# Delta rule of a decoder step: the scale rows of k and q go through DRAM instead of one-hot products

## The chip, the cores and the metric

The kernel runs on one core of a Trainium2 chip. The metric is the device time of one execution in microseconds (us); the kernel is timed several times and the median is given. One execution was taken by the hardware profiler. In the profile PE is TensorE's matmul stream, PEld its weight loads, DVE is VectorE, ACT ScalarE, POOL GpSimd and SP SyncE, which issues most of the transfers (SPq in the rows is its queue, POOLq that of GpSimd). 1% of the time is about 19 us.

## The reference, cut to what matters

One step of a two-layer decoder for a prompt of 256 tokens and 32 sample tokens (8 requests of 4). Each layer has a token mixer with three branches, of which one is a gated delta rule with 8 heads; the lines that matter here scale k and q by one number for each token and head:

```
q = l2norm(qkv[:, :, 0]) * (DN_DK ** -0.5)
k = l2norm(qkv[:, :, 1])
...
kb = kc * bc[..., None]
a_mat = jnp.einsum('bihd,bjhd->bhij', kb, kc) * jnp.where(strict, decay, 0.0)
...
q_dec = jnp.moveaxis(qc * jnp.exp(gcum)[..., None], 1, 2)
scores = jnp.einsum('bihd,bjhd->bhij', qc, kc) * decay
```

## The kernel before, in words

Activations lie with channels on the 128 partitions and the T = 288 tokens (256 and 32) in the free dimension. Nearly all the work is projections: 128x128 weight tiles, each split into a high and a low part, so that a tile is three products with 288 columns. These are the rows `mmps<-xh,wh`, `mmps<-xl,wh` and `mmps<-xh,wl`. Four tiles form one block: SP loads it (`wr<-in_wst`, 256 KB, 6 buffers), ACT writes its high part (`wh<-wr`), DVE its low part (`wl<-wr,wh`), two blocks ahead of TensorE; `wh` and `wl` have 4 buffers. A layer has 450 blocks.

Everything else is written as generators that run in the background: each time that a block begins (`w`, `tick`), the first two generators of a list advance to their next `yield`; `yield n` sits out n of these turns. A scheduler then gives every engine a fixed order of instructions, with waits for data and for free buffers. Tiles of 128x288 (`self.A`) come from one pool of 50 buffers.

The delta rule of four heads is one generator, `dn_mix(hf)`, with hf = 0 and 1, so four passes in two layers. Here they are called pass 0 and pass 1 of a layer. A pass first has its eight scale factors for each token and head in a tile with tokens on partitions (`TK`), turns them by transposes into 32 rows of 288 tokens (`rows`), copies these to SBUF (`fr`, `stack`) and splits them into two parts in a 128-partition tile (`st`, shown as `dst`). Rows h, 4 + h and 8 + h are the factors of k, of q and of the decayed q of head h; row 12 + h holds the summed log decay.

To multiply a head's k (128 channels x 288 tokens) by a row of tokens, the row has to stand on all partitions. `bcast` does that with a product: the stationary operand is one column of a one-hot matrix, repeated 128 times, the moving one is `st`, and the result is a PSUM tile `rowbc` with the row on every partition. DVE then multiplies k or q by it (`kq<-k,rowbc`, `kq<-q,rowbc`, `qd<-q,rowbc`). `kq`, with one buffer, is the moving operand of the products `pk`. Each of four heads has three such products and one of the same form for row 12 + h, which a mask product (`rowbc<-msk,idb`) is added to and ACT exponentiates (`et`, `eg`). PSUM tiles for all of this come from five banks (`self.X`).

Of the kernel before, what the change touches and what calls it, by code (L numbers as in the profile page):

```python
# [8 lines left out]
F32 = mybir.dt.float32  # L9
# [8 lines left out]
P = 128  # L18
TP = 256
TS = 32  # L20
T = TP + TS
# [204 lines left out]
class Net:  # L226
# [344 lines left out]
    def spread(self, r, w=72):  # L571
        bc = self.X("bc")
        for g in range(4):
            self.mmul(bc[:, w * g:w * g + w], self.ident[:, 32 * g:32 * g + 1].to_broadcast([P, P]), r)
        return bc
# [232 lines left out]
    def stack(self, psrow, n, tag, bufs, again=False):  # L808
        st = self.St[tag]
        s0 = st  # L810
        if again:
            st = s0[:, 128:128 + T]
        fr = self.A(nm="fr")[0:32]
        fs = self.R([32, 32], tag + "s", bufs=bufs)
        if n < 32:
            self.nc.gpsimd.memset(fr, 0.0)
        self.cp(fr[0:n], psrow[0:n, 0:T])
        self.cp(st[0:32], fr)
        self.tt(st[32:64], fr, st[0:32].bitcast(F32), ALU.subtract)
        self.pcp(fs, fr[:, 256:288])  # L820
        if again:
            self.vcp(s0[0:64, 0:128], st[0:64, 128:256].bitcast(F32))
        return s0, fs

    def bcast(self, st, m):
        ps = self.X("rowbc")
        self.mmul(ps[:, 0:T], self.e32[:, m:m + 1].to_broadcast([P, P]), st)
        return ps


    def dn_proj(self, hf, xs, out):
# [13 lines left out]
    def dn_mix(self, hf, q, k, v):  # L845
# [46 lines left out]
        ps = self.X("vtr")  # L892
# [5 lines left out]
        rows = self.X("rows")  # L898
        for c in range(2):
            self.tp(rows[0:32, c * 128:c * 128 + 128], TK[:, c].rearrange("p a h -> p (a h)"))  # L900
        self.mmul(rows[0:32, 256:288], TK[0:32, 2].rearrange("p a h -> p (a h)"), self.ident[0:32, 0:32])
        st, fr = self.stack(rows, 32, "dst", 1)
        yield 1
        ps = self.X("vtr")
        for h in range(4):
            self.tp(ps[:, h * 128:h * 128 + 128], v[h][:, 128:256])
        for h in range(4):
            self.act(r4(vb[1])[:, h], r4(ps)[:, h], AF.Copy, scale=TK[:, 1, 6, h:h + 1])
        yield

        av = lambda t: t.rearrange("p (a i) -> p a i", a=2)
        m = self.M(1024, nm="asc")
        ASC = [[av(self.A(nm="asc")[:, 0:256]) for _ in range(4)], [av(m[:, i * 256:i * 256 + 256]) for i in range(4)]]
        asc = lambda c, h: ASC[c][h]
        QD = self.R([P, 4, 160], "qd")
        KQ = self.R([P, 4, 2, 32], "kqs")
        EG = self.R([P, 4, 9], "eg", bufs=2)
        for h in range(4):
            kq = self.R([P, 2, T], "kq")
            b0 = self.bcast(st, h)  # L920
            self.tt(kq[:, 0, :], k[h], b0[:, 0:T])
            b1 = self.bcast(st, 4 + h)
            self.tt(kq[:, 1, :], q[h], b1[:, 0:T])
            gb = self.X("rowbc")
            sel = self.e32[:, 12 + h:13 + h].to_broadcast([P, P])

            self.mmul(gb[:, 0:T], sel, st, True, False)
            self.mmul(gb[:, 0:256], self.idb, self.MK("mk3")[:, 0:256], False, True)
            et = self.S(256, "et")
            for c in range(2):  # L930
                self.act(et[:, c * 128:c * 128 + 128], gb[:, c * 128:c * 128 + 128], AF.Exp,
                         bias=G[:, 5, c, hf * 4 + h:hf * 4 + h + 1])
            self.act(EG[:, h, 0:1], gb[:, 255:256], AF.Exp)
            self.act(EG[:, h, 1:9], gb[:, 256:288].rearrange("p (b s) -> p b s", s=4)[:, :, 3], AF.Exp)
            yield
            b2 = self.bcast(st, 8 + h)
            self.tt(QD[:, h], q[h][:, 128:288], b2[:, 128:288])
            pk = self.X("pk")
            pkv = pk.rearrange("p (c a i) -> p c a i", c=2, a=2)
            for c in range(2):  # L940
                self.mmul(pkv[:, c], k[h][:, c * 128:c * 128 + 128], kq[:, :, c * 128:c * 128 + 128])
            for c in range(2):
                self.stt(asc(c, h), pkv[:, c], TK[:, c, 4, h:h + 1],
                         et[:, c * 128:c * 128 + 128].unsqueeze(1).to_broadcast([P, 2, P]))
            self.pcp(KQ[:, h], kq[:, :, 256:288])
            yield
# [4 lines left out]
        for b in range(2):  # L951
            ps = self.X("atr")
# [36 lines left out]
        for c in range(2):  # L989
            ps = self.X("ktr")  # L990
# [87 lines left out]
        ps = b4()  # L1078
# [5 lines left out]
        ps = b4()  # L1084
# [8 lines left out]
        for j in range(2):  # L1093
            po = self.X("po").rearrange("p (h t) -> p h t", h=2)
            for i in range(2):
                h = 2 * j + i
# [5 lines left out]
        ps = b4()  # L1102
# [13 lines left out]
        ps = self.X("on")  # L1116
# [225 lines left out]
    def ssm_rows(self):  # L1342
        G = self.gtok
        while (self.l, "scalars") not in self.done:
            yield
        rows = self.X("rows")
        for c in range(2):
            self.tp(rows[0:16, c * 128:c * 128 + 128], G[:, 0, c, 8:24])
        self.mmul(rows[0:16, 256:288], G[0:32, 0, 2, 8:24], self.ident[0:32, 0:32])
        st, fr = self.stack(rows, 16, "sst", 1, again=True)  # L1350
        el = self.S(8, "sel")
        yield
        ea = self.X("ea")
        for g in range(4):
            self.mmul(ea[32 * g:32 * g + 32, 0:16], fr[0:16], self.C("i32")[0:16, 0:16])
        EA = self.R([P, 16], "sea")
        self.act(EA, ea[:, 0:16], AF.Exp)
        self.act(el[0:16], fr[0:16].rearrange("p (b s) -> p b s", s=4)[:, :, 3], AF.Exp)
        yield
        ed = self.S(128, "eld")[0:16].rearrange("p (b h) -> p b h", b=NB)  # L1360
        self.tt(ed, el[0:16].unsqueeze(2).to_broadcast([16, NB, 16]),
                self.C("i32")[0:16, 0:16].unsqueeze(1).to_broadcast([16, NB, 16]))
        yield
        elp = self.X("elp")
        self.mmul(elp[:, 0:128], self.ones[0:16], ed)
        EL = self.R([P, NB, 16], "sel2")
        self.cp(EL, elp[:, 0:128].rearrange("p (b h) -> p b h", b=NB))
        self.sst = (st, EA, EL)
# [704 lines left out]
```

## Time and profile before

| | us |
|---|---|
| median of 3 runs | 1889.24 |
| lowest and highest | 1888.33, 1892.48 |
| the profiled execution, its own time | 1886.77 |
| span of the profiled execution, first to last instruction | 1884.9 |
| PE busy | 1857.6 (99%) |
| DVE busy | 1404.7 (75%) |
| ACT busy | 1126.6 (60%) |
| POOL busy | 307.2 (16%) |

The mean granted clock of TensorE is 0.998 of full speed. The 1.9 us between time and span lie around the span. A matmul's row lasts longer than the distance to the next one's start, since matmuls overlap: what one costs is read from the starts.

### The profile page before, as it was taken

The numbers are of one execution on the slowest core, as the hardware profiler recorded it, in microseconds if no ns is written. First come the engines' busy times: TensorE is split into PE (matmuls) and PEld (weight loads), VectorE is DVE, ScalarE is ACT, GpSimd is POOL, SyncE is SP. The second block draws the span as 40 slices with busy tenths as digits, with TensorE's granted clock in tenths as the row PEclk, the third lists the DMA queues.
The fourth block names the chain that finished last, engine by engine and source line by source line (L and its number), as shares of the span: only waits on it lengthen the run. The fifth ranks groups of instructions, "written<-read, shape, count | busy, mean of one in ns | idle before, by whom it ended". The sixth has DMA issues, their size and how long they took to land. (4 is left out here: it accounts for less than half of the span.)

```text
span 1884.9 us, 44571 instructions
## 1 busy us (share of the span) xinstructions
PE 1857.6 (99%) x16446; PEld 1733.4 (92%) x16446; DVE 1404.7 (75%) x3153; ACT 1126.6 (60%) x2735; POOL 307.2 (16%) x777
## 2 busy tenths in 40 slices
PE   9999999999999999999999999999999999999998
PEld 8998999988999989999999889989889999899997
DVE  6978767677978768766588785777688887587665
ACT  6666665655546457756466756656655465476563
POOL 3533212332000000000024232123210000000000
PEclk9999999999999999999999999999999999999999
DMA  7545446588554684766556453465876556747663
GB/s 257 173 147 170 120 118 196 164 286 275 186 172 145 206 289 138 239 202 205 152 158 182 121 180 111 132 200 158 294 265 187 171 171 208 253 153 239 213 191 98
DMA packets 184442, 354.52 MB, mean 188 GB/s; under 512 B 30688, under 2 KB 42144, under 8 KB 184224
## 3 DMA queue, kind: packets, MB, share of 16 engines
q1 hardware_dynamic: 176320, 326.44, 55.6%
q0 software_dynamic: 7904, 25.23, 3.8%
q8 instruction: 129, 2.11, 0.5%
q14 instruction: 89, 0.73, 0.1%
HBM read 316.54 MB, written 35.05 MB: 187 GB/s over the span
## 5 line engine op out<-in xcount | busy, mean ns | idle before, releaser
L294 ACT CAST wh<-wr 128x512 fp32r<-128x512 f32 x900 | 555.4, 620 | 553.5 <-PE mmps L286 467.7
L303 DVE TENSOR_TENSOR wl<-wr,wh 128x512 fp32r<-128x512 f32 x900 | 619.2, 691 | 285.0 <-ACT wh L294 272.2
L286 PE MATMUL mmps<-xh,wh 128*128 128x288 f32 x2400 | 725.7, 305 | 4.3 <-DVE xh L307 1.8
L286 PE MATMUL mmps<-xl,wh 128*128 128x288 f32 x2400 | 712.2, 297 | 0.0
L286 PE MATMUL mmps<-xh,wl 128*128 128x288 f32 x2400 | 709.2, 296 | 0.2 <-DVE wl L303 0.2
L286 PEld LDWEIGHTS mmps<-xh,wh 128*128 128x128 f32 x2400 | 450.6, 189 | 24.2 <-issue 12.3
L286 PEld LDWEIGHTS mmps<-xl,wh 128*128 128x128 f32 x2400 | 453.1, 189 | 9.0 <-issue 5.6
L286 PEld LDWEIGHTS mmps<-xh,wl 128*128 128x128 f32 x2400 | 452.4, 188 | 6.4 <-issue 3.8
L286 PE MATMUL mmps<-prs,wh 128*128 128x288 f32 x1280 | 260.5, 297 | 0.7 <-ACT prs L294 0.6
L286 PEld LDWEIGHTS mmps<-prs,wh 128*128 128x128 f32 x1280 | 205.3, 188 | 2.2 <-ACT prs L294 0.9
L286 PE MATMUL mmps<-prs,wl 128*128 128x288 f32 x640 | 188.5, 295 | 0.0
L312 DVE SCALAR_TENSOR_TENSOR cy<-cb,cwh,cy 128x312 f32<-128x312 f32 x240 | 129.5, 540 | 19.8 <-ACT cy L291 13.5
L286 PEld LDWEIGHTS mmps<-prs,wl 128*128 128x128 f32 x640 | 120.7, 189 | 0.0
L286 PE MATMUL mmps<-ph,wh 128*128 128x288 f32 x256 | 76.4, 298 | 0.0
L286 PE MATMUL mmps<-pl,wh 128*128 128x288 f32 x256 | 75.7, 296 | 0.0
L286 PE MATMUL mmps<-ph,wl 128*128 128x288 f32 x256 | 75.6, 295 | 0.0
L331 POOL DMA_DIRECT2D out_osd<-dnu x32 | 17.3, 542 | 338.6 <-DVE dnu L312 330.3
L300 POOL COPY cvp<-cb 128x3 f32<-128x3 f32 x80 | 29.6, 370 | 214.0 <-ACT cb L294 213.8
L291 ACT ACTIVATE ct<-cy 128x312 f32<-128x312 f32 x80 | 37.3, 466 | 37.8 <-DVE cy L312 34.3
L286 PEld LDWEIGHTS mmps<-ph,wh 128*128 128x128 f32 x256 | 48.1, 188 | 2.1 <-ACT b L294 0.8
L286 PEld LDWEIGHTS mmps<-pl,wh 128*128 128x128 f32 x256 | 48.1, 188 | 0.8 <-issue 0.4
L286 PEld LDWEIGHTS mmps<-ph,wl 128*128 128x128 f32 x256 | 48.1, 188 | 0.4 <-issue 0.4
(509 smaller groups left out, 2941.4 us busy)
## 6 DMA issues: line engine op xcount, KB each, us to landing
wr<-in_wst SPq DMA_DIRECT2D x900, 256.0 KB
kc<-in_k SPq DMA_DIRECT2D x28, 512.0 KB
kc<-in_v SPq DMA_DIRECT2D x28, 512.0 KB
dns<-in_dns SPq DMA_DIRECT2D x16, 512.0 KB
h<-in_h SPq DMA_DIRECT2D x16, 512.0 KB
out_oss<-h POOLq DMA_DIRECT2D x16, 512.0 KB, 3.8
kc<-in_km SPq DMA_DIRECT2D x16, 512.0 KB
kc<-in_vm SPq DMA_DIRECT2D x16, 512.0 KB
```

The lines of the kernel that those rows point to most:

```text
L286: self.nc.tensor.matmul(out, lhsT, rhs, start=start, stop=stop)
L291: return self.nc.scalar.activation(out, in_, func, **k)
L294: self.nc.scalar.copy(out, in_)
L300: self.nc.gpsimd.tensor_copy(out, in_)
L303: self.nc.vector.tensor_tensor(out, a, b, op=op)
L312: return self.nc.vector.scalar_tensor_tensor(out, a, s, b, op0=op0, op1=op1)
L331: self.nc.gpsimd.dma_start(out=out, in_=in_)
```

## The change

`bcast` is gone. After `stack` (which now also returns `fr`) the first 12 rows of `fr` are stored to a DRAM tile `dr` by POOL's queue, and each row is loaded from there with a source step of 0 over the partitions, so that all 128 partitions of an SBUF tile `rb` get the same 1152 bytes. `spread(h)` issues the three loads of head h: those of heads 0 and 1 ahead of the loop over heads, those of heads 2 and 3 in the turns of heads 0 and 1. DVE's three multiplications read `rb` in SBUF instead of `rowbc` in PSUM. The fourth product, for the log decay, stays. Ahead of the loop, `yield` becomes `yield 1`: the loop starts one turn, so one block, later.

```diff
-    def bcast(self, st, m):
-        ps = self.X("rowbc")
-        self.mmul(ps[:, 0:T], self.e32[:, m:m + 1].to_broadcast([P, P]), st)
-        return ps
...
-        st, fr = self.stack(rows, 32, "dst", 1)
+        st, fr, full = self.stack(rows, 32, "dst", 1)
+        dr = self.pd.tile([12, T], F32, tag="dr", name="dr")
+        self.store(dr, full[0:12])
+        rb = {}
+
+        def spread(h):
+            for m in range(h, 12, 4):
+                rb[m] = self.A(nm="rb")
+                self.load(rb[m], bass.AP(dr.tensor, dr.offset + m * T, [[0, P], [1, T]]))
         yield 1
+        spread(0)
         ps = self.X("vtr")
...
-        yield
+        spread(1)
+        yield 1
...
-            b0 = self.bcast(st, h)
-            self.tt(kq[:, 0, :], k[h], b0[:, 0:T])
-            b1 = self.bcast(st, 4 + h)
-            self.tt(kq[:, 1, :], q[h], b1[:, 0:T])
+            self.tt(kq[:, 0, :], k[h], rb.pop(h))
+            self.tt(kq[:, 1, :], q[h], rb.pop(4 + h))
...
-            b2 = self.bcast(st, 8 + h)
-            self.tt(QD[:, h], q[h][:, 128:288], b2[:, 128:288])
+            self.tt(QD[:, h], q[h][:, 128:288], rb.pop(8 + h)[:, 128:288])
+            if h < 2:
+                spread(h + 2)
```

TensorE's order in pass 0 of layer 1, at the turn from head 0 to head 1. Before:

```order
L286 MATMUL mmps<-xh,wh 128x288
L286 MATMUL mmps<-xl,wh 128x288
L286 MATMUL pk<-kq,k 128x256 x2
L286 MATMUL rowbc<-dst,e_439 128x288 x3
L286 LDWEIGHTS idb
L286 MATMUL rowbc<-msk,idb 128x256
L286 MATMUL mmps<-xh,wl 128x288
```

The same place in the order of the change:

```order
L286 MATMUL mmps<-xh,wl 128x288
L286 MATMUL pk<-kq,k 128x256 x2
L286 MATMUL rowbc<-dst,e_439 128x288
L286 LDWEIGHTS idb
L286 MATMUL rowbc<-msk,idb 128x256
L286 MATMUL mmps<-xh,wh 128x288
```

Two of the three products with `dst` are gone here (the third, for the decayed q, stood alone further down and is gone too). The first `rowbc` of the pass now stands 5 projection products later than before, and 33 projection products lie between it and head 0's `pk`; before it was 19, with one more `rowbc` among them.

VectorE's order at head 0 of the same pass. Before:

```order
L303 TENSOR_TENSOR dst<-fr,dst 32x288
L312 SCALAR_TENSOR_TENSOR cy<-cb_125,cwh,cy 128x312
L303 TENSOR_TENSOR wl<-wr,wh 128x512
L312 SCALAR_TENSOR_TENSOR cy<-cb_125,cwh,cy 128x312
L303 TENSOR_TENSOR wl<-wr,wh 128x512
L303 TENSOR_TENSOR kq<-k,rowbc 128x288
L312 SCALAR_TENSOR_TENSOR k<-ct,cy 128x256
L303 TENSOR_TENSOR kq<-q,rowbc 128x288
L303 TENSOR_TENSOR wl<-wr,wh 128x512
L303 TENSOR_TENSOR qd<-q,rowbc 128x160
```

And in the change:

```order
L303 TENSOR_TENSOR dst<-fr,dst 32x288
L312 SCALAR_TENSOR_TENSOR cy<-cb_125,cwh,cy 128x312
L303 TENSOR_TENSOR wl<-wr,wh 128x512
L312 SCALAR_TENSOR_TENSOR cy<-cb_125,cwh,cy 128x312
L303 TENSOR_TENSOR wl<-wr,wh 128x512
L312 SCALAR_TENSOR_TENSOR k<-ct,cy 128x256
L303 TENSOR_TENSOR wl<-wr,wh 128x512 x3
L303 TENSOR_TENSOR kq<-k,rb 128x288
L303 TENSOR_TENSOR kq<-q,rb 128x288
L303 TENSOR_TENSOR wl<-wr,wh 128x512
L303 TENSOR_TENSOR qd<-q,rb 128x160
```

The two multiplications of head 0 have moved behind three more `wl` of later blocks.

SyncE's queue in the same pass; before, 21 weight loads stood in one run here:

```order
L328 DMA wr<-in_wst 128x512 x12
L328 DMA rb<-dr 128x288 x6
L328 DMA wr<-in_wst 128x512 x3
L328 DMA rb<-dr 128x288
L328 DMA wr<-in_wst 128x512
L328 DMA rb<-dr 128x288 x2
L328 DMA wr<-in_wst 128x512 x2
L328 DMA rb<-dr 128x288 x2
L328 DMA wr<-in_wst 128x512
L328 DMA rb<-dr 128x288
```

The twelve loads of a pass stand between weight loads, six of them in one run.

## Rows read from the trace of the kernel before

**Rows 1.** The page: busy time, share of the span and instructions.

```profile
PE 1857.6 (99%) x16446; PEld 1733.4 (92%) x16446; DVE 1404.7 (75%) x3153; ACT 1126.6 (60%) x2735; POOL 307.2 (16%) x777
```

**Rows 2.** Waits on TensorE, all places: us, times, longest.

```profile
PE rowbc L286 <- DVE dst L303: 0.4, 2, 0.2
```

**Rows 3.** Layer 1's passes 0 and 1: PE, PEld, DVE, ACT, POOL, clock, DMA, GB/s.

```profile
141.00:165.00 24.00, 23.60 (x166) 22.00 (x165) 21.91 (x56) 17.34 (x55) 9.12 (x26) 1.00 0.39 114
262.00:286.00 24.00, 23.84 (x171) 21.94 (x170) 19.09 (x50) 13.93 (x47) 5.24 (x12) 1.00 0.40 119
```

**Rows 4.** Instructions on tile rowbc: durations min/median/max in ns.

```profile
L286 PE MATMUL rowbc<-dst,e x64: 288/294/482, 146.5 to 1216.8; 128*128 128x288 f32 x64
L303 DVE TENSOR_TENSOR kq<-k,rowbc x16: 439/454/455, 148.6 to 1214.5; 128x288 f32<-128x288 f32 x16
```

**Rows 5.** Timeline of PE, pass 0 of layer 1, head 2: start, length.

```profile
155.19 0.29 PE L286 MATMUL mmps<-xh,wl 128*128 128x288 f32 x1
155.32 0.56 PE L286 MATMUL rowbc<-dst,e 128*128 128x288 f32 x3
155.72 0.28 PE L286 MATMUL rowbc<-msk,idb 128*128 128x256 bf16 x1
...
157.42 0.30 PE L286 MATMUL rowbc<-dst,e 128*128 128x288 f32 x1
157.56 1.02 PE L286 MATMUL pk<-kq,k 128*128 128x256 f32 x4
```

**Rows 6.** Timeline of PE at head 0 of layer 1's passes 0 and 1.

```profile
146.02 0.29 PE L286 MATMUL mmps<-xh,wh 128*128 128x288 f32 x1
146.51 0.67 PE L286 MATMUL rowbc<-dst,e 128*128 128x288 f32 x3 [0.21 <-DVE dst L303]
...
264.37 0.29 PE L286 MATMUL mmps<-xh,wl 128*128 128x288 f32 x1
264.82 1.10 PE L286 MATMUL pk<-kq,k 128*128 128x256 f32 x4 [0.15 <-DVE sst L297]
```

**Rows 7.** Timeline of ACT and POOL in pass 0 of layer 1.

```profile
144.25 0.39 ACT L294 COPY fr<-rows 32x288 f32<-32x288 f32 x1
...
144.81 0.20 POOL L300 COPY dsts<-fr 32x32 f32<-32x32 f32 x1
```

**Rows 8.** The DMA view and tile xd: us from issue to landing (last number).

```profile
out_ocs<-cvo POOLq DMA_DIRECT2D x4, 144.0 KB, 2.1
...
out_ocp<-cvp POOLq DMA_DIRECT2D x8, 6.0 KB, 3.5
...
DMA to landing us min/median/max: 2.0/4.0/6.3
```

**Rows 9.** Timeline of SP's queue and ACT at the kernel's start.

```profile
1.18 0.42 SPq L328 DMA_DIRECT2D x<-in_x  x1
1.65 0.42 SPq L328 DMA_DIRECT2D wr<-in_wst  x1
...
3.90 0.53 ACT L291 ACTIVATE xh<-x,prm 128x288 fp32r<-128x288 f32 x1 [1.57 <-DMA x<-in_x]
```

**Rows 10.** Timeline of DVE at head 0, pass 0 of layer 1.

```profile
146.95 0.69 DVE L303 TENSOR_TENSOR wl<-wr,wh 128x512 fp32r<-128x512 f32 x1
...
148.01 0.69 DVE L303 TENSOR_TENSOR wl<-wr,wh 128x512 fp32r<-128x512 f32 x1
148.61 0.45 DVE L303 TENSOR_TENSOR kq<-k,rowbc 128x288 f32<-128x288 f32 x1
149.00 0.43 DVE L312 SCALAR_TENSOR_TENSOR k<-ct,cy 128x256 f32<-128x256 f32 x1
149.35 0.45 DVE L303 TENSOR_TENSOR kq<-q,rowbc 128x288 f32<-128x288 f32 x1
```

**Rows 11.** What SP's queue waits for, the longest: us, times, longest.

```profile
SPq L328 <- DVE wl L303: 1033.2, 697, 11.2
```

**Rows 12.** Instructions on tile kqs: POOL's copies of kq.

```profile
L300 POOL COPY kqs<-kq x16: 236/636/1196, 149.9 to 1215.4; 128x64 f32<-128x64 f32 x16
```

More of the change, by code (lines that the diff above doesn't have):

```diff
@@ L822, in stack @@
             self.vcp(s0[0:64, 0:128], st[0:64, 128:256].bitcast(F32))
-        return s0, fs
-    def bcast(self, st, m):
-        ps = self.X("rowbc")
-        self.mmul(ps[:, 0:T], self.e32[:, m:m + 1].to_broadcast([P, P]), st)
-        return ps
+        return s0, fs, fr
     def dn_proj(self, hf, xs, out):
@@ L1349, in ssm_rows @@
         self.mmul(rows[0:16, 256:288], G[0:32, 0, 2, 8:24], self.ident[0:32, 0:32])
-        st, fr = self.stack(rows, 16, "sst", 1, again=True)
+        st, fr, _ = self.stack(rows, 16, "sst", 1, again=True)
         el = self.S(8, "sel")
```

## The prediction

> **What bounds the kernel now.** The page comes first: TensorE is busy 99% of the span, DVE 75%, ACT 60% [rows 1]. In the four passes of the delta rule, the only stretches that the change edits, it is no different: TensorE is busy 23.60 of 24 us in pass 0 and 23.84 in pass 1 [rows 3]. DVE has 21.91 and 19.09 us of work there, so in pass 0 it is close behind. The transfer engines are at 39 and 40% of their time. So what leaves TensorE's queue should shorten the time one for one, as long as nothing new makes it wait.
>
> **What is removed.** The trace has 64 products `rowbc<-dst,e` [rows 4]. Four heads in four passes keep one each, 16, so 48 go. Their row says 294 ns each, but that is a length, not a price, since the next product starts long before the end. Read the starts instead: at head 2 three of them start from 155.32, and the mask product follows at 155.72, so 0.40 / 3 = 0.133 us each; the lone one at 157.42 is followed at 157.56, 0.14 [rows 5]. An ordinary projection product takes the same: 155.19 to 155.32. Price: 48 x 0.133 = **6.4 us**. By the length it would be 48 x 0.294 = 14.1 us; that would be right only if products didn't overlap, and these starts show that they do. I take 6.4.
>
> Two waits go as well. In pass 0 the first of these products starts 0.49 us after the projection product ahead of it, where 0.13 is the rule: 0.36 lost, because DVE has not finished `dst` [rows 6], and this happens once in each layer [rows 2]. The changed order puts the first `rowbc` 5 projection products later, by which time (146.02 + 6 x 0.13 = 146.8) `dst` is there. That is 2 x 0.36 = **0.7 us**. In pass 1, head 0's `pk` starts 0.45 after the product ahead [rows 6], 0.32 lost, since DVE multiplies q only after work on another task's `sst`. In the changed order both multiplications of head 0 stand ahead of that: 2 x 0.32 = **0.6 us**. Lower bound for both together nothing, upper 1.3; I take 1.3, since in both cases the order itself moves the two apart.
>
> **What is added, and what covers it.** DVE multiplies the same number of elements, and I price that at no change: 454 ns for the 288 columns of `kq` with one operand in PSUM [rows 4], and a `wl` with both operands in SBUF has 512 columns in 0.69 us [rows 10], no more for a column. POOL gets four stores, one in each pass, and works 9.12 of 24 us in pass 0 [rows 3]. SP gets 48 issues of about 0.47 us (1.18 to 1.65 [rows 9]), 5.6 us in each pass; it mostly waits for buffers anyway, 1033 us of the span for DVE's `wl` alone [rows 11]. The transfers: in pass 0 the engines moved 114 GB/s x 24 us = 2.74 MB in 0.39 x 24 us x 16 = 150 engine-us, 18 KB per engine-us. A load writes 128 x 1152 B = 147 KB, so 8.1 engine-us or 0.5 us of all 16. Twelve take 6 us of 24, which brings the share from 0.39 to 0.64: still free time. That the extra turn (`yield 1`) makes each pass end one block later I price at nothing; the next tasks in the built program's order keep 3 blocks of margin to the place that needs the delta rule's result, where they had 4. If that cover were gone it would cost about a block of 12 products, 1.6 us, for each pass.
>
> **The one new wait that can reach TensorE** is the round trip in pass 0, so I follow it by hand. `fr` ends at 144.64, POOL's copy of it starts at 144.81 and takes 0.20 [rows 7], so the store is issued at about 145.0. Small stores of POOL land 2.1 to 3.5 us after issue [rows 8]: 147.1 to 148.5. In the changed order SP has by then a weight load to issue that waits for the `wl` of 146.95, done at 147.64 [rows 10], so the first load leaves at about 148.0 to 148.5. A load of the same shape, 128 x 288, took 1.18 to 3.90 = 2.72 us from issue to its first reader [rows 9], and the second one leaves 0.47 later: the rows for k and q are there at 150.7 to 151.2 and 151.2 to 151.7. DVE meanwhile: after the `wl` of 148.01 (0.60 to the next start) come `k` (0.35) and three `wl` (0.6 each) [rows 10], so its `kq` would start at 150.8, the second at 151.2, done at 151.6 by itself, or 152.1 with the late bound of the load. TensorE wants head 0's `pk` after 146.8, plus 0.26 for `rowbc` with its mask, plus 33 x 0.13: at about 151.4. So `pk` is 0.2 to 0.7 us late. At heads 1 to 3 DVE runs a denser list, and the later loads wait for buffers that DVE frees one head earlier; I allow as much again there. For the two passes 0 that is 2 x 0.65 = **1.3 us** lost; bounds 0 and, with the slowest store of 6.3 us [rows 8], `pk` at 151.3 + 2.72 + 0.47 + 0.5 = 155.0, 3.6 late, 7.2 for both layers. In pass 1 the built order has more than five blocks (8 us) between the transposes that make the rows and head 0's `pk`, so I price the trip there at nothing. Behind DVE's waiting `kq` stand the next `wl`, which TensorE wants two blocks (3 us) later, so a wait of up to that length does no further harm.
>
> On SP weight loads stand behind the six `rb` that wait for the store. With six buffers a load is issued when the split six blocks back ends; five blocks at 2.1 us (1884.9 / 900) less 2.72 for landing leave some 7.7 us, against a delay of 1 to 3. No loss.
>
> **Sum:** -6.4 - 1.3 + 1.3 = -6.4 us. The profiled execution's own time would go from 1886.8 to 1880.4; its span is 1.9 shorter. That execution is 2.5 below the median of the runs, so against the median I expect 1889.24 - 6.4 = **1882.8**. About 0.2%, 3.8 us, is what a measurement of this kernel can tell from no change.
>
> **Rivals.**
> (a) The round trip decides: the store lands as late as the slowest of `xd`, `pk` waits 3.6 in both passes 0, 7.2 in all. For: the median of those sixteen stores is 4.0, not 2.1 [rows 8]. Against: they were issued eight in a row, this one stands alone. Time 1889.24 - 7.7 + 7.2 = 1888.7.
> (b) DVE is the real bound of pass 0 (21.91 of 24). Then the products removed there give nothing and only pass 1 and its wait pay: 24 x 0.133 + 0.6 = 3.8, 1885.4. Against: TensorE, not DVE, is busy 98% there.
> (c) DVE's multiplications, now with both operands in SBUF, and POOL's copies hold each other up. For: POOL's `kqs` copies of 64 columns take 236 to 1196 ns [rows 12], so something stretches them. If each head of pass 0 lost the median of 0.64, that is 8 x 0.64 = 5.1: 1882.8 + 5.1 = 1887.9. [...]
> (d) Slower: the 128 reads of one 1152-byte row hurt. No row of this trace repeats a source. The engines have 61% of 24 us free, 14.6 us; twelve loads of 8 rows for each engine fit as long as a row takes under 0.15 us (by the share above it takes 0.06). SP's weight loads can be late by 7.7 more. So from about 0.23 us a row on, weights come late; at 0.3 us it is 28.8 - 14.6 - 7.7 = 6.5 us in each of four passes, 26 - 7.7: about 1908.
>
> **Chances.** Forecast 0.62, (a) 0.13, (b) 0.10, (c) 0.07, (d) 0.08. Faster takes the forecast, half of (b), which lies on the line, and a little of (a) and (c): 0.69. Slower is (d) and a tail of (a): 0.09. The rest, 0.22, is no change. The likeliest case alone spans 1880 to 1885.5; the range goes from all waits removed and nothing added, with 2 us for neighbours that shift (1879), to (a) (1889).
>
> **What would show it.** `rowbc<-dst,e` x16 in place of x64; TensorE's busy time lower by about 14 (lengths) but the span by about 6; no wait for `dst` in pass 0; a wait of `pk` for DVE's `kq` of some tenths of a us in pass 0 and none in pass 1; no wait for DMA `wr` on ACT that was not there. If the span shrinks by far less than 6 while `pk` waits for `kq`, and DVE for the `rb` load, it was (a); if `kq` rows last far over 454 ns, (c); if `wh` waits for `wr`, (d). What would make it wrong altogether is a reshuffled neighbour: later tasks shift by a block and some wait elsewhere grows by a few us.

## The result: slower by 0.7%, and the profile after

| | before | after |
|---|---|---|
| median, us | 1889.83 (4 runs) | 1901.79 (4 runs) |
| lowest and highest | 1888.33, 1892.48 | 1900.78, 1903.65 |
| span of the profiled execution | 1884.9 | 1899.0 |
| mean granted clock of TensorE | 0.998 | 0.995 |

The ratio is 1.0067, 95% interval 1.0054 to 1.0079: 10 to 15 us slower, outside the range of the prediction and on the other side of no change. The page of the change, first part, answers to [rows 1], and a line of the tile view for `rowbc` to [rows 4]:

```profile
PE 1857.2 (98%) x16398; PEld 1729.3 (91%) x16398; DVE 1406.7 (74%) x3153; ACT 1127.2 (59%) x2735; POOL 309.0 (16%) x781
```

```profile
L286 PE MATMUL rowbc<-dst,e x16: 288/346/592, 148.6 to 1228.1; 128*128 128x288 f32 x16
```

48 products are gone, and yet the span is 14.1 us longer. TensorE waits where it did not; the waits of TensorE in the changed kernel (us in total, times, longest):

```profile
PE sw L286 <- POOL tsd L300: 6.6, 4, 2.0
PE pk L286 <- DVE kq L303: 4.8, 4, 1.7
PE bc L286 <- DVE rms L312: 2.9, 4, 1.0
PE ea L286 <- POOL ssts L300: 2.9, 2, 1.7
PE t L289 <- DVE s L307: 2.7, 4, 1.3
PE mpo L286 <- DMA kc<-in_vm: 2.2, 4, 0.7
PE mmps L286 <- ACT wh L294: 2.0, 2, 1.0
PE mmps L286 <- DVE xh L307: 1.9, 5, 0.4
PE sqk L286 <- DMA kc<-in_k: 1.7, 2, 1.4
```

Before, the same view had 3.2 for `sw`, 1.5 for `t`, 1.8 for `mpo`, 1.5 for `wh`, and no row for `pk` on `kq`, `ea` or `sqk`. The waits for `dst` [rows 2] and of `pk` for `sst` [rows 6] are gone, as forecast.

The second loss shows in no wait. Stretches of the changed kernel, with layer 1's passes ahead (columns as in [rows 3]; the third last is the granted clock):

```profile
142.70:166.70 24.00, 20.68 (x143) 18.64 (x142) 19.45 (x48) 15.25 (x46) 9.37 (x24) 1.00 0.60 170
262.00:286.00 24.00, 22.04 (x148) 19.90 (x146) 16.27 (x44) 13.14 (x43) 3.29 (x11) 0.93 0.58 183
185.00:190.00 5.00, 3.07 (x16) 2.79 (x18) 1.77 (x4) 1.18 (x6) 1.96 (x5) 0.78 0.84 309
190.00:195.00 5.00, 5.00 (x83) 4.01 (x82) 3.30 (x14) 1.59 (x4) 0.87 (x3) 0.88 0.34 107
275.00:280.00 5.00, 5.00 (x20) 4.11 (x20) 2.92 (x10) 2.50 (x13) 0.68 (x2) 0.66 0.82 258
1125.00:1130.00 5.00, 3.17 (x15) 2.94 (x14) 2.07 (x4) 1.08 (x5) 2.33 (x5) 0.65 0.86 260
1130.00:1135.00 5.00, 5.00 (x53) 3.81 (x51) 2.51 (x11) 1.27 (x3) 0.87 (x3) 0.67 0.44 164
```

In the last five rows TensorE's granted clock is 0.65 to 0.88; us by us it is 1.00 up to 187, 276 and 1126, and 0.50 from 188 to 191, 277 to 279 and 1127 to 1133. The rows lie behind three waits of 1.7 to 2.0 us: `ea` at 274.6, shown below, and these two of `sw`:

```profile
186.93 0.49 PE L286 MATMUL sw<-tsd,skvs 128*128 128x128 f32 x2 [2.03 <-POOL tsd L300]
...
1127.30 0.79 PE L286 MATMUL sw<-tsd,skvs 128*128 128x128 f32 x2 [1.83 <-POOL tsd L300]
```

From 275 to 280 it is busy for all 5 us and gets 20 matmuls done. With length times (1 - clock) as an estimate of what a stretch loses, at most, the five lose 5 x (0.22 + 0.12 + 0.34 + 0.35 + 0.33) = 6.8 us. Before, one such stretch in the layers' work lost 1.7:

```profile
1115.00:1120.00 5.00, 4.42 (x48) 4.06 (x50) 1.81 (x4) 1.52 (x6) 0.81 (x4) 0.66 0.79 306
```

The order is the same in all four places (before, `sw` at 1115.58 waits 1.62): TensorE begins to wait, then the clock falls, to 0.50 at its lowest in each. Whether the wait makes it fall, these rows alone do not show.

The sum: -6.4 for the products; +4.8 `pk`, +2.9 `ea`, +3.4 `sw`, +1.7 `sqk`, +1.2 `t`, +2.2 for `wh`, `mpo` and some smaller ones; -1.5 for the waits that went or shrank; +5.1 at most at the lower clock. That is 13.4 of the 14.1 measured.

How a row comes late: timeline of POOL, SP's queue, DVE and TensorE in layer 1, pass 0 and then pass 1.

```profile
146.74 0.56 POOL L331 DMA_DIRECT2D dr<-fr  x1
...
149.97 2.71 SPq L328 DMA_DIRECT2D rb<-dr  x6
...
153.07 0.46 DVE L303 TENSOR_TENSOR kq<-k,rb 128x288 f32<-128x288 f32 x1
...
154.61 0.46 DVE L303 TENSOR_TENSOR kq<-q,rb 128x288 f32<-128x288 f32 x1 [1.08 <-DMA rb<-dr]
...
155.13 1.13 PE L286 MATMUL pk<-kq,k 128*128 128x256 f32 x4 [1.28 <-DVE kq L303]
...
156.99 0.33 SPq L328 DMA_DIRECT2D rb<-dr  x1
...
161.83 0.46 DVE L303 TENSOR_TENSOR kq<-k,rb 128x288 f32<-128x288 f32 x1 [1.26 <-DMA rb<-dr]
...
163.30 1.13 PE L286 MATMUL pk<-kq,k 128*128 128x256 f32 x4 [1.65 <-DVE kq L303]
...
260.29 0.52 POOL L331 DMA_DIRECT2D dr<-fr  x1
...
262.26 4.74 SPq L328 DMA_DIRECT2D wr<-in_wst  x3
...
267.16 3.15 SPq L328 DMA_DIRECT2D rb<-dr  x5
...
271.47 0.46 DVE L303 TENSOR_TENSOR kq<-k,rb 128x288 f32<-128x288 f32 x1 [1.59 <-DMA rb<-dr]
...
273.01 0.33 POOL L816 MEMSET fr<- 32x288 f32 x1 [4.27 <-DVE kq L303]
...
274.32 0.20 POOL L300 COPY ssts<-fr 32x32 f32<-32x32 f32 x1
...
274.58 0.25 PE L286 MATMUL ea<-cst,ssts 16*32 16x16 f32 x8 [1.72 <-POOL ssts L300]
```

In pass 0 the first row takes at most 3.1 us from issue to DVE, which was busy until then; the second, behind it in a run of six, takes 154.61 - 150.42 = 4.2, and head 2's first one 4.8. In pass 1 the store is issued at 260.3, but the loads stand in SP's queue behind three weight loads and leave 6.9 us later; in e13, e16 and e18 below, where they wait for the store alone, it is 3.9, so the place in the queue costs 3.0. DVE waits for the row, POOL waits for DVE, and TensorE stands at `ea`, a product of another branch.

### The profile page after: what moved, and what is told of

It is laid out like the page before. It is cut to its first block, busy times and chain, and to the rows that moved or that the text cites. A ratio compares the mean times of both kernels' runs of the same rounds, so it can differ in the third digit from the quotient of the medians.

```text
span 1899.0 us, 44603 instructions
## 1 busy us (share of the span) xinstructions
PE 1857.2 (98%) x16398; PEld 1729.3 (91%) x16398; DVE 1406.7 (74%) x3153; ACT 1127.2 (59%) x2735; POOL 309.0 (16%) x781
```

## The experiments

All ratios are to the kernel before on the same chip. Its medians there were 1889.5 to 1890.0 us, so a difference between two rows of medians can be off by about half a us from this alone. Two theories at the start: **S**, the later turn moves neighbours; **L**, the loads cost. Later ones are in the expectations.

| run | median, us | ratio, 95% interval |
|---|---|---|
| e1 later turn alone | 1889.81 | 1.0005 (0.9993 to 1.0016) |
| e2 change, no later turn | 1897.63 | 1.0041 (1.0027 to 1.0056) |
| e3 change, no loads | 1885.33 | 0.9978 (0.9969 to 0.9988) |
| e4 change, no loads, no later turn | 1880.52 | 0.9954 (0.9938 to 0.9969) |
| e5 before, with loads | 1901.30 | 1.0060 (1.0047 to 1.0073) |
| e6 rows earlier | 1889.71 | 1.0001 (0.9992 to 1.0010) |
| e7 one buffer moved | 1900.01 | 1.0060 (1.0045 to 1.0074) |
| e8 rows of the decayed q only | 1889.02 | 0.9996 (0.9987 to 1.0004) |
| e9 rows earlier, three big loads | 1884.35 | 0.9976 (0.9964 to 0.9989) |
| e10 rows earlier, all loads ahead | 1884.28 | 0.9967 (0.9954 to 0.9980) |
| e11 before, with loads into DRAM | 1889.90 | 0.9998 (0.9987 to 1.0008) |
| e12 change, waits of sw filled | 1896.45 | 1.0033 (1.0019 to 1.0048) |
| e13 change, three big loads | 1885.19 | 0.9979 (0.9969 to 0.9988) |
| e14 e9, waits of sw filled | 1881.97 | 0.9962 (0.9950 to 0.9975) |
| e15 before, waits of sw filled | 1888.74 | 0.9996 (0.9987 to 1.0004) |
| e16 change, one load for a head | 1901.59 | 1.0061 (1.0044 to 1.0078) |
| e17 e16, small copies on DVE | 1893.36 | 1.0022 (1.0012 to 1.0031) |
| e18 e16, loads on POOL's queue | 1907.97 | 1.0091 (1.0075 to 1.0108) |

### Turn and products: e1 to e4

e1 against before; e2 is the change with this line as it was. e3 and e4 are the change with and without that line, with the store and the loads left out and the rows replaced by a constant tile, so the scale factors are missing from what they compute:

```diff
-        yield
+        yield 1
...
+        cs = self.z3[:, 0:T]
...
-            self.tt(kq[:, 0, :], k[h], rb.pop(h))
+            self.tt(kq[:, 0, :], k[h], cs)
```

> The kernel before with one line of the change: the delta rule's loop over heads starts one turn later. No load, no store, all 64 products. Theory S (the later turn puts the delta rule's small tasks among other tasks on DVE and POOL, and TensorE waits for them): in the trace of the change the waits for tsd grew by 3.4 us, for s by 1.2, for kc by 1.7, others by 0.8, about 7 us, and TensorE's clock fell to half three times where it fell once before; so 5 to 11 us over the kernel before, 1895 to 1901. Theory L (only the loads cost something, the turn is free, as the prediction had it): 1889 to 1891.

> The change without the later turn: the rows come by DMA, the loop starts in the turn in which it started before. Theory S: the waits for tsd, s and kc fall back to those of before, the wait of pk for kq grows by up to a block (2.1 us) in each pass, 8 in all; together about 1895 to 1904, and the wait for ssts stays or grows. Theory L: one turn less lead and nothing given back, 1904 to 1910.

> The change with the store and the loads left out: k and q are multiplied by a constant tile that lies in SBUF, so the scale factors are left out of the computation; 48 products fewer, later turn kept. Theory S: the 6.4 to 7.7 us of the prediction are gained and the turn's 5 to 11 lost: 1887 to 1894, with sw waiting for tsd 6 us. Theory L: 1881 to 1884.

> As the run before, without the later turn: what the 48 products are worth when nothing else moves (the scale factors are left out). Both theories: 48 x 0.133 = 6.4 us and up to 1.3 of waits, 1882 to 1884. A third theory, that TensorE does not bound the passes and DVE does, gives 1886 or more.

e4: the products and the wait for `sst` are worth 1889.47 - 1880.52 = 9.0 us (by the ratio 5.9 to 11.7), a little more than the 7.7 forecast, though the wait for `dst` is still there; TensorE did bound the passes. e1: the turn alone costs nothing that can be told, so S in its simple form falls, though `sw` waits more:

```profile
PE sw L286 <- POOL tsd L300: 5.5, 4, 1.4
```

(3.2 before; but the waits for `dst` and `sst`, 0.7, are gone, and this trace has no stretch at the lower clock in the layers' work.) With the products gone the turn does cost, 1885.33 - 1880.52 = 4.8 us: in e3 `sw` waits 5.9 us against 3.2 in e4, `sqk` 1.3 against none, and a stretch at the lower clock behind `sw` (180 to 190) costs at most 1.8. With the loads in, it gives no gain: e2 is 4 us below the change. There `sw` is back at 3.2 and `sqk` does not wait, but `pk` waits 8.1 and `t` 4.5. The loads cost 17.1 us without the turn (e2 - e4) and 16.5 with it (after - e3). So neither theory holds alone: e2 came out in the range of S, e3 between the two, and what the loads cost is the larger part. Why they cost it is the question.

### Transfers, buffers, lead: e5 to e11

e5 adds the change's stores and loads to the kernel before and keeps the products. e11 differs from it in one line, e7 from the change in one:

```diff
-                rb[m] = self.A(nm="rb")
+                rb[m] = self.pd.tile([P, T], F32, tag="rb", name="rb", bufs=12)
...
-        fr = self.A(nm="fr")[0:32]
+        fr = (self.S(T, "fr") if again else self.A(nm="fr"))[0:32]
```

> The kernel before, all 64 products kept, with the four stores and 48 loads of the change added at the places where it has them (no later turn); nobody reads the loaded rows. Theory W (what costs is that kq, and so pk, waits for the rows): the transfers by themselves cost nothing, 1888 to 1892. Theory C (the transfers cost in another way: they delay weight loads in SP's queue, fill the transfer engines, or hold buffers that others want): 1894 or more, with waits for wh or for buffers that were not there.

> As e5 (the kernel before with all its products, and the stores and 48 loads added), but the loads go to tiles in DRAM that nobody reads, so they take no buffer in SBUF; queue, places and bytes are those of e5. Theory B (e5's 11.8 us come from buffers that are handed on only when the load has landed, as its waits of asc and vT for rb show): 1888 to 1892. Theory C (the transfers themselves, by SP's queue or by the engines): 1896 to 1902.

> The change with one buffer moved: the 16 rows that the state space branch copies to SBUF (fr of sst) take a tile of another pool. In the change that tile is one that a loaded row had, so POOL's memset of it waits until DVE has multiplied with that row, and ea waits for POOL, 2.9 us in the two layers, with a stretch at half clock behind the first one. If the handed-on buffer is the cause: the wait of ea for ssts goes, and 2.9 to 5 us with it: 1896 to 1899. If POOL's late copies come from POOL's order alone: 1900 to 1903 with the wait of ea as it was.

The issues and the traffic cost nothing that can be told: e11 stays at 1.000 (its loads land in DRAM; e13 below brings the same bytes into SBUF at no cost either). e5's 12 us come from the buffers. A tile that nobody reads is handed on at once, and its next writer waits for the landing; DVE's and ACT's waits in e5:

```profile
DVE asc L312 <- DMA rb<-dr: 10.7, 7, 3.0
...
ACT vT L294 <- DMA rb<-dr: 6.2, 2, 3.9
```

In the change the tiles have readers, and one handed-on buffer is seen to hold up TensorE there: `fr` of the state space branch, whose memset waits 4.27 us above. e7 moves it; the wait of `ea` is gone, but the time falls by 1.8 us only, less than the 2.9 to 5 expected and with intervals that overlap: `t` waits 1.9 longer and `pk` 0.7.

e6 makes the rows two turns earlier, and the loop starts when it did before; e10 also issues all loads ahead of the loop and takes e7's line; e9 loads four rows at once. e8 loads only the rows of the decayed q. First the move of e6 (the first transposes of v now stand behind the rows), then e9's load, with `a` = 0 to 2 for the rows of k, q and the decayed q (e10 keeps the small ones), then e8's line:

```diff
-        yield 2
-        ps = self.X("vtr")
-        for h in range(4):
-            self.tp(ps[:, h * 128:h * 128 + 128], v[h][:, 0:128])
...
-        yield
+        yield 1
         rows = self.X("rows")
...
+            self.tp(ps[:, h * 128:h * 128 + 128], v[h][:, 0:128])
...
+        yield
+        spread(1)
+        ps = self.X("vtr")
...
-            for m in range(h, 12, 4):
-                rb[m] = self.A(nm="rb")
-                self.load(rb[m], bass.AP(dr.tensor, dr.offset + m * T, [[0, P], [1, T]]))
+            t = self.M(nm="rb")
+            self.load(t, bass.AP(dr.tensor, dr.offset + 4 * a * T, [[0, P], [1, 4 * T]]))
...
-            if h < 2:
-                spread(h + 2)
...
-            for m in range(h, 12, 4):
+            for m in (8 + h,):
```

> The change with the same transfers, but the rows are made two turns earlier, ahead of the first transposes of v, and stored and loaded from there; the loop over heads starts in the turn in which it started in the kernel before. Five turns, some 10 us, lie between the rows and head 0 where the change has four. Theory W: head 0 and 1 no longer wait, heads 2 and 3 (whose loads leave in the turns of heads 0 and 1) may still, by 1 to 2 us a pass; from the 1880.5 us of the run without loads that is 1882 to 1889. Theory C: the transfers cost what they cost in the change, 17 us over the run without loads: 1893 to 1898.

> As e6, but all twelve loads of a pass are issued ahead of the loop over heads (six with the first transposes of v, six one turn later), and the rows of the state space branch take a tile of the other pool as in e7. If only lead and that one buffer are missing in e6: pk and ea no longer wait, 1881 to 1885. If twelve buffers at once make others wait (50 tiles in all): ACT and DVE wait for buffers, 1886 to 1893. If six loads in a run delay weights: waits for wh of some us.

> The rows are made two turns earlier as in e6, and each load brings four rows at once (those of k, of q, or of the decayed q for all four heads: 128 x 4608 B) into a tile of another pool (9 buffers of 1152 numbers): three loads for a pass in place of twelve, all ahead of the loop, and no buffer of the 50 is used. If what is left in e6 (pk waits 4.9 us, ea 1.0) comes from late and many small loads and from the handed-on buffers, nothing waits for a row: 1880.5 us of the run without loads plus at most 3: 1881 to 1884. If the broadcast transfers cost by their mere presence in SP's queue or the transfer engines: 1887 to 1892, with waits for wh.

> Only the four rows of the decayed q of each pass come by DMA (16 loads and 4 stores in the kernel, 16 products fewer), k's and q's keep their products, no later turn. qd is not an operand of pk, so no product of the loop waits for it. Theory W: 16 x 0.133 = 2.1 us gained, 1885 to 1888. Theory C with a cost in proportion to the loads: 17 x 16 / 48 = 5.7 lost against 2.1 to 3 gained: 1891 to 1894.

e6 gives back 12 us of the change's loss and ends level with before, just above its range: `pk` still waits 4.9 us, 1.1 of it at heads 0, 2 and 3 of layer 1's pass 0 and 3.5 at heads 0 and 3 of layer 2's, so head 0 waits after all. e10 and e9 load everything ahead of the loop; `pk` waits 1.2 and 1.5, and both beat the kernel before, by the ratio by 6.2 and 4.5 us. e9 still waits 2.2 us at `ea`, e10, with e7's line, not at all. e8 comes out 0.5 us lower, too little to tell, where 2.1 was expected.

### The lower clock: e12, e14, e15

Products without data fill TensorE's wait: 16 ahead of each `sw` of the change (e12), 14 in the passes 0 of e9 (e14) and of before (e15).

```diff
+        self.warm(16)
         ps = self.X("sw")
         self.mmul(ps[:, 0:128], kv[:, 0], self.tsd)
```

> The change, with 16 products that need no data (128x256, about 1.7 us) ahead of sw in the four places where TensorE waits 1.4 to 2.0 us for tsd, so that it works there in place of waiting. If the stretches at half clock behind these places follow from the wait, the clock stays whole there: of the 5 us by which the change loses more to half clock than the kernel before, 3 to 4 come back: 1898 to 1900. If the clock falls for another reason: 1901 to 1905 and the same stretches.

> e9 with 14 products that need no data (about 1.5 us) ahead of sw in pass 0 of each layer, where TensorE waits 1.6 us for tsd in the kernel before as well, and where a stretch at half clock follows in some traces and not in others. If the wait brings the stretch: 1 to 3 us less than e9, 1881.5 to 1883.5, and a narrower spread of the runs. If the clock there has another reason: 1884 to 1885.5.

> The kernel before with the same 14 products ahead of sw in pass 0 of each layer, to tell what of e14 is the clock's alone: 1 to 3 us less than the kernel before if the wait brings the stretch at half clock (1886.5 to 1889), no change or up to 0.5 more if not. The distance to e14 should stay that of e9 to the kernel before, about 5 us.

e12 does 64 products more than the change and is 5.3 us faster, more than the 3 to 4 expected. Its stretches, three of those shown above:

```profile
185.00:190.00 5.00, 4.45 (x47) 3.53 (x46) 3.68 (x11) 2.44 (x9) 3.28 (x8) 1.00 0.62 183
190.00:195.00 5.00, 5.00 (x80) 4.28 (x81) 2.87 (x14) 1.80 (x7) 1.08 (x3) 1.00 0.77 240
1125.00:1130.00 5.00, 4.93 (x53) 4.06 (x54) 2.57 (x6) 2.28 (x8) 3.09 (x7) 1.00 0.90 296
```

`sw` waits 0.3 us in all here, and TensorE is at full clock where it was not; the mean granted clock of its five runs is 0.997 to 0.999, that of the change's four 0.994 to 0.995. At `sw` the wait brings the lower clock: the three stretches have 1.00 in place of 0.78, 0.88 and 0.65. Not all of the 5.3 is the filling's: the waits of `ea` fell as well, from 2.9 to 1.3 us, and the stretch behind the first of them is gone. In e14 and e15 the step is 2.4 and 1.2 us, with intervals that overlap those without the filling, and that of e15 holds 1: the direction fits, a gain is not shown. e14 still lost 3.4 us at the lower clock behind other waits (`ea`, `mpo`).

### What makes the rows late, and who stands behind: e13, e16 to e18

e13 is the change, turn included, with e9's three loads, all in the two turns ahead of the loop. e16 leaves each load in its turn and brings a head's three rows at once into the same pool. e17 moves two small copies (`kqs`, shown, and `z`) off POOL in e16, e18 the loads to POOL's queue.

```diff
+            t = self.M(nm="rb")
+            self.load(t[:, 0:3 * T], bass.AP(dr.tensor, dr.offset + h * T, [[0, P], [4 * T, 3], [1, T]]))
...
-            self.pcp(KQ[:, h], kq[:, :, 256:288])
+            self.vcp(KQ[:, h], kq[:, :, 256:288])
...
-            self.load(t[:, 0:3 * T], bass.AP(dr.tensor, dr.offset + h * T, [[0, P], [4 * T, 3], [1, T]]))
+            self.store(t[:, 0:3 * T], bass.AP(dr.tensor, dr.offset + h * T, [[0, P], [4 * T, 3], [1, T]]))
```

> The change with its later turn and its place for the rows, but three loads of four rows in tiles of the other pool (as e9): none of the 50 buffers is taken, and the rows of heads 2 and 3 are loaded ahead of the loop. If handed-on buffers make most of the change's loss, it comes near the run without loads that keeps the turn (e3, 1885.3): 1885 to 1889. If the late rows of heads 0 and 1 do: pk waits 3 us or more and a half-clock stretch or two follow, 1892 to 1898.

> The change with its turn and with each load in its place (heads 0 and 1 ahead of the loop, 2 and 3 in the turns of heads 0 and 1), but the three rows of a head come by one load into one tile of the other pool (four loads for a pass, none of the 50 buffers). If handed-on buffers make most of the change's loss: near e13, 1885 to 1889. If it is that the rows of heads 2 and 3 are loaded late (in e13 they were ahead of the loop): pk waits 1 to 2 us at these heads in each layer, with half clock behind, 1891 to 1897.

> e16 with the two small copies of a pass that read what the loaded rows gave (kqs and z, for the sample tokens) on DVE in place of POOL. In e16 these stand ahead of the state space branch's fr and ssts in POOL's fixed order, and ea waits 7.5 us in the two passes 1 with 3 and 6 us at half clock behind. If a late row costs most by what is queued behind its readers on POOL: the wait of ea goes and 10 to 14 us with it, 1887 to 1892. If TensorE then waits as long for kq itself: 1896 to 1902.

> e16 with the row loads issued by POOL behind the store, not by SP behind weight loads. In e16 the first load of pass 1 leaves SP at 262.59, 3.9 us after the store was issued, with a weight load ahead of it, and DVE has the rows at 268.4. If SP's queue makes the rows late: kq starts 2 us or more earlier in pass 1 and ea waits less: 1890 to 1897. If the time goes in the transfers (5.9 us from issue to the reader) or in POOL, which then waits for its own store: 1898 to 1904.

e13 is level with e3, which has no loads at all: the whole 16.5 us are gone, with the change's turn and place of the rows kept. I took that for the buffers; e16 refuted it. It uses none of the 50 buffers either, and the loss is back in full, above both ranges. Nor does `pk` wait at heads 2 and 3, as the other theory had it: it waits 2.3 us at head 0 of the passes 0, and `ea` waits 7.5 in the passes 1. Pass 1 of layer 1 in e13, then in e16:

```profile
258.68 1.28 SPq L328 DMA_DIRECT2D rb<-dr  x3
...
262.76 0.48 DVE L303 TENSOR_TENSOR kq<-k,rb 128x288 f32<-128x288 f32 x1 [1.23 <-DMA rb<-dr]
...
263.30 0.63 POOL L300 COPY ssts<-fr 32x32 f32<-32x32 f32 x1
265.30 0.64 POOL L300 COPY kqs<-kq 128x64 f32<-128x64 f32 x1 [1.37 <-DVE kq L303]
```

```profile
262.59 0.91 SPq L328 DMA_DIRECT2D rb<-dr  x2
...
268.44 0.46 DVE L303 TENSOR_TENSOR kq<-k,rb 128x288 f32<-128x288 f32 x1 [3.02 <-DMA rb<-dr]
...
269.33 0.63 POOL L300 COPY kqs<-kq 128x64 f32<-128x64 f32 x1 [10.10 <-DVE kq L303]
269.91 0.33 POOL L816 MEMSET fr<- 32x288 f32 x1
...
271.09 0.25 PE L286 MATMUL ea<-cst,ssts 16*32 16x16 f32 x8 [3.01 <-POOL ssts L300]
```

and, in layer 2's pass 1 of e16, the other wait of `ea`, then the stretches around and behind it, columns as above:

```profile
1211.56 0.30 PE L286 MATMUL ea<-cst,ssts 16*32 16x16 f32 x8 [4.53 <-POOL ssts L300]
```

```profile
1210.00:1215.00 5.00, 3.44 (x17) 2.65 (x18) 3.39 (x10) 2.23 (x9) 1.66 (x7) 0.51 0.89 297
1215.00:1220.00 5.00, 5.00 (x18) 4.27 (x18) 2.41 (x7) 2.18 (x8) 0.23 (x1) 0.50 0.29 75
```

In both runs the first load leaves 3.9 us after the store was issued. In e13 it needs 4.1 us to DVE, in e16 5.9. And in e16's POOL order `kqs`, which waits for the row, stands ahead of `fr` and `ssts`; in e13, as in the kernel before, it stands behind them. e17 takes that copy (and `z`) off POOL, with DVE paying for them: 8.2 us come back (7.4 by the ratios, where 10 to 14 were expected), and `ea` has no wait left. What remains is `pk` with 3.5, and 3.3 at `elp`, whose operand DVE makes behind the waiting `kq`:

```profile
PE elp L286 <- DVE eld L303: 3.3, 2, 1.6
```

e18 went the wrong way, above both ranges. POOL waits 3.35 us for its own store before it can issue, again 3.9 after the store was issued, and the first load then needs 6.0 us, so in e16 SP's queue did not make the first row late:

```profile
261.29 2.30 POOL L331 DMA_DIRECT2D rb<-dr  x3 [3.35 <-DMA dr<-fr]
...
267.25 0.46 DVE L303 TENSOR_TENSOR kq<-k,rb 128x288 f32<-128x288 f32 x1 [3.03 <-DMA rb<-dr]
```

Whether the size of the pieces makes the difference is not shown: a load is 576 KB in e13, in pieces of 4608 B, with 4.1 us, and 432 KB in e16, in pieces of 1152 B, with 5.9, but the traffic beside them differs too.

## Why the prediction was wrong, point by point

In medians: the products brought -9.0 us (e4), the later turn +4.8 (e3 - e4) and the loads +16.5 (the change - e3), 12.3 in all, where 12.0 were measured. The prediction had -7.7, nothing and +1.3.

- **The products.** Right: 6.4 + 1.3 forecast, 9.0 measured in e4 (5.9 to 11.7). The turn, not the products, moved `dst` away: in e2 and e4, without it, the wait for `dst` is there. The two waits are 0.7 us in the trace's own rows (0.4 and 0.3), where the prediction read 1.3 from the starts. The sign "busy time lower by about 14" was wrong in itself: overlapping rows count once, and it fell by 9.4 in e4 and, with the lower clock, by 0.4 in the change.
- **The step that failed: the two round trips.** "I allow as much again there", 1.3 us for the passes 0, and "in pass 1 ... I price the trip there at nothing". In layer 1 the first load left when forecast (149.97; 148.0 to 148.5 plus the 1.8 us by which this trace runs later at `dsts`), and its row was in time. But I gave every load 2.72 us, the figure of a lone one at the kernel's start [rows 9]; the second took 4.2, the first ones of heads 2 and 3 4.8 and 3.9. `pk` waits 4.8 us in the passes 0, at heads 0 and 2, between the 1.3 forecast and the 7.2 of rival (a), whose reason, a store as late as 6.3 us, did not occur: the stores of `dr` landed in 1.7 to 4.0. In layer 1's pass 1, 11.2 us lie between the issue of the store and head 0's `kq` (260.29 to 271.47): 3.9 for the store, 3.0 in SP's queue, 4.3 for the load. The 1033 us that SP waits for buffers [rows 11] I read as free time, but a load behind a waiting weight load waits with it, 3.0 us here. `pk` itself does not wait there; TensorE stops ahead of it, at `ea`.
- **Who is queued behind.** I named what stands behind the waiting `kq` on DVE, where nothing was lost, and not what waits on POOL for `kq`. There the copies `kqs` and `z` and a handed-on buffer stand ahead of `ssts`: `ea` waits 2.9 us in the change, and taking the two copies off POOL is worth 8.2 from e16 to e17.
- **The later turn at nothing.** Right by itself (e1, 0.3 us more), wrong with the products gone: 4.8 us (e3 - e4). The margin of blocks that I checked was that of the pass's result, not that of the small tasks behind it. In layer 1's pass 0 the last `siv` of DVE waits 0.7 us for ACT, the four copies `tsd` behind it take 2.1 us where they took 1.5, and `sw` waits for them. What delays the load that `sqk` waits for was not followed.
- **The clock had no term.** Every new wait was priced at its own length. The lower clock behind three waits added at most 5.1 us, and the run that fills four waits got 5.3 back (e12).
- **DVE, transfers, weights.** Right: `kq` lasts 455 to 457 ns (454 before), the transfer engines are at 0.60 in pass 0 (0.64 forecast), TensorE waits 0.5 more for `wh`, and e11 is level. So (d) falls, and (b) with the 9.0 of e4. For (c), no run shows that DVE and POOL hold each other up: `kq` kept its length, and POOL's `kqs` became shorter, with a median of 238 ns in place of 636 [rows 12]; but it is 238 in e1 too, where DVE still reads PSUM.
- **The last sentence** of the prediction, a reshuffled neighbour, was part of it; it carried no chance of its own. The sign given for (a), `pk` behind `kq` and DVE behind the `rb` load, did come, but with 4.8 of the 19 us above the forecast, and from the loads, not from the store.

Open: how the late rows' time divides between small pieces, six loads in a run and the weight loads beside them. A version with all twelve small loads ahead of the loop at the change's place was not tried.

## What to carry to other kernels

A new transfer in a kernel with fixed orders was late here by the whole chain: store, place in the issuing queue, landing among its neighbours (3.9, 3.0 and 4.3 us in layer 1's pass 1). Give it the lead of that chain, not of a lone load, ahead of the loop: three large loads (e9) or twelve small ones (e10) were then 4 to 6 us faster than before. Then follow the wait past its reader: every engine that waits for that reader has a queue of its own, and TensorE may stop at a product of another branch (here `ea`, for 1.72 us). Price a wait of TensorE of some 2 us with the lower clock behind it (at most 3.4 us behind the 1.83 of `sw`), and fill it if it can't be removed (e12, which fills four, was 5.3 us faster, not by that alone).

## What the runs showed that was not expected

Behind waits of 1.3 to 2.0 us TensorE's granted clock fell in some places and executions and not in others (it stayed at 1.00 behind `pk`'s 1.65 at 163.3 and fell to 0.50 behind `ea`'s 1.72; behind `ea`'s 1.33 in e14 it is 0.66 from 1195 to 1200); what followed one wait cost at most 3.4 us in the change (1125 to 1135), and 5.0 at e16's wait of 4.53. POOL's copies of `kq` took a median of 636 ns before and 238 in the change. Where DVE's operand lies does not explain it: they took 238 in e1, which reads PSUM, and 560 in e6, which reads SBUF. What does was not tried.
